# A fourth k chunk with seven products in eight late pairs, and an added transfer for two weight halves of each

## The chip, the cores and the metric

The kernel runs on one core of one Trainium2 chip. The metric is the device time in microseconds of one execution. The kernel before took 1013.76, 1014.27 and 1014.4 us in three runs, median 1014.27 us.

## The reference

The program is one layer of a bidirectional encoder on `x` of 256 x 2048 float32 (batch 1). The normalised input is multiplied with one wide weight `w_in`, whose columns are cut into the parts of two branches and two gates; each branch is projected by a 2048 x 2048 weight, the two are merged by the gates, and an output projection and a last RMSNorm follow:

```python
h = _rms_norm(x, norm_g)
proj = jnp.einsum('bsd,dn->bsn', h, w_in.astype(h.dtype))
...
q_p, k_p, v_p, o_p, za_p, gif_p, xb_p, zb_p, ga_p, gb_p = jnp.split(proj, cuts, axis=-1)
ya = _mlstm_branch(q_p, k_p, v_p, o_p, za_p, gif_p, b_if, head_g)
yb = _rglru_branch(xb_p, zb_p, conv_w, conv_b, w_rg, b_rg, lam)
ya = jnp.einsum('bsw,wd->bsd', ya, w_branch_a.astype(ya.dtype))
yb = jnp.einsum('bsw,wd->bsd', yb, w_branch_b.astype(yb.dtype))
merged = (jax.nn.sigmoid(ga_p.astype(jnp.float32)) * ya.astype(jnp.float32)
          + jax.nn.sigmoid(gb_p.astype(jnp.float32)) * yb.astype(jnp.float32)).astype(x.dtype)
return x + jnp.einsum('bsd,de->bse', merged, w_out.astype(x.dtype))
```

What concerns the change are five products of a 256 x 2048 activation with 2048 x 2048 weights late in the program: `yb @ w_branch_b`, the gates `gb` and `ga` (columns of `w_in`), `ya @ w_branch_a`, and then `merged @ w_out`.

## The kernel before, in words

**Products in two parts.** A float32 operand is kept as two tiles of the type that TensorE multiplies here: `hi` (the rounded value) and `lo` (the value less `hi`). A product is three matmuls, a·hi, a·lo and b·hi, where a and b are the activation's two parts. Each is 128 x 128 by 128 x 512.

**A plain chunk.** A weight block has 512 columns and eight k chunks of 256 rows (`KC` = 2 tiles of 128). `load_chunk` (L125) brings one chunk of a block, 128 x 1024 or 512 KB, on SyncE's queue (L134) to a `raw` tile of six, ScalarE casts it to `whi` (L140), and VectorE subtracts to `wlo` (L141). Each has four buffers. A plain chunk of one block is 12 matmuls, two k tiles by two row blocks by three; one of both blocks is 24.

**A pair.** `pair` (L163) computes two blocks at once. Its eight matmul groups end in two accumulators of two PSUM banks each (`acc`). At some k chunks, the "product" chunks, `products` (L184) forms quarter sums of the four 256 x 256 sub-blocks by VectorE (L199, L200, L203, L204) and does seven products in place of eight, 21 matmuls in place of 24. Three products go straight to the accumulators and four to extra banks, `aux` p1, p5, p7 and p6, which hold sums over all product chunks of the pair. The transfers of such a chunk are L190 and L191, its casts L180, its low halves L181. Beside the weights it needs "forms", the same quarter sums of the activation, made ahead by `make_form` (L271 to L285) into slots of SBUF. Which chunks are products and at which of the eight places they are worked is given by the tables `S_..` and `L_..`.

**The end of a pair.** When the last product chunk is done, the aux banks are combined in the result tile: ScalarE copies p1 (L252), then VectorE adds p6 (L253), p7 (L254) and p5 twice (L255, L256). L253 needs both p6 and the copy of p1. The plain chunks left over follow, first all of the first half, then of the second. After each half VectorE adds its accumulator (L262), and what the pair is for follows (for a gate a sigmoid on ScalarE, then a multiply at L957; for the last pairs L988 and L989). [...]

**The eight late pairs.** They are, in order: `wb` twice (WB0, WB1 here), gate b twice (GB0, GB1), gate a twice (GA0, GA1) and `wa` twice (WA0, WA1). Each has three product chunks, kq 0, 2 and 4 at places 0, 2 and 4 (in WA1 at 1, 3 and 5), so 3 x 21 + 5 x 24 = 183 matmuls. After the last product chunk three plain chunks of each half are left over (two in WA1). Then comes `block_nat` (L145) for `wo[2]`, a block alone, whose chunks are preceded by transposes of the merged result (L981) with their low half by VectorE (L336), then a pair for `wo[0]` and `wo[1]` with four product chunks, and `wo[3]`.

**What sets the order.** The instructions of one engine run in the order in which the tile scheduler put them, each after the semaphores of what it reads and of the buffer that it overwrites. `with urgent()` gives the loads, casts and evictions a higher priority. A row that waits on its engine holds up all rows behind it.

## Time and profile before

| | |
|---|---|
| times | 1013.76, 1014.27, 1014.4 us, median 1014.27 us |
| profiled execution | span 1012.2 us from the first to the last instruction, 2.1 us less than the median |
| TensorE busy | 1003.0 us, 99% |
| VectorE busy | 875.8 us, 87% |
| ScalarE busy | 628.6 us, 62% |
| GpSimd busy | 18.6 us, 2% |
| 16 DMA engines of q1, where the weights come in | 58.9% |
| mean granted TensorE clock | 0.998 |
| start of L253, the first add of the aux banks, in WB0, WB1, GB0, GB1, GA0, GA1, WA0, WA1 | 607.9, 649.9, 691.3, 732.9, 774.3, 815.3, 856.8, 905.2 us |
| start of L253 in the pair of `wo` | 978.3 us |

Busy shares are of the whole span. In the names of a row, what is written stands left of the arrow and what is read right of it, each a tile's name; the shapes are partitions x elements. A slot's tile is named for the slot (sE, sD), an accumulator acc, an extra bank aux. Consecutive rows of one engine overlap a little: an instruction's duration is longer than the distance to the next one's start.

### The profile page before, as it was taken

Reading aid. Unit: us, or ns where it says so; the run is one execution under the profiler, and the core shown is the slowest. Engines: PE = TensorE matmul, PEld = TensorE weight load, DVE = VectorE, ACT = ScalarE, POOL = GpSimd, SP = SyncE. Lnnn points to the kernel's source line nnn. Section 1 sums busy time; section 2 is a strip of 40 time slices with the busy share of each in tenths; the row PEclk is TensorE's granted clock in tenths of the full one; section 3 lists DMA queues with packets and bytes.
Section 4 is the critical chain, followed back from the end, with each engine's and each line's share of the span. In section 5 each row is a group of like instructions: output and inputs, shape, how many; then the busy total and the mean of one; then the engine's idle time right before and its main releaser. Section 6 shows DMA issues by size and latency. Waiting matters only on the chain.

```text
span 1012.2 us, 13718 instructions
## 1 busy us (share of the span) xinstructions
PE 1003.0 (99%) x5045; PEld 853.2 (84%) x5045; DVE 875.8 (87%) x1167; ACT 628.6 (62%) x825; POOL 18.6 (2%) x37
## 2 busy tenths in 40 slices
PE   9999999999999999999999999999999999999997
...
DVE  6687898889769888997697888998898988999996
...
GB/s 349 263 208 157 160 153 198 173 213 197 167 190 167 177 197 184 210 167 227 146 199 208 155 208 188 212 212 201 187 216 200 219 177 212 184 217 336 161 200 83
DMA packets 56387, 199.32 MB, mean 197 GB/s; under 512 B 6400, under 2 KB 7424, under 8 KB 55936
## 3 DMA queue, kind: packets, MB, share of 16 engines
q1 hardware_dynamic: 55456, 197.13, 58.9%
...
## 4 chain that ended last, share of the span: by engine, by line
PE 97%; DVE 1%; DMA 1%; ACT 0%; issue 0%; ACTq 0%; SPq 0%; DVEq 0%
PE acc L176 17%; PE acc L177 17%; PE acc L174 17%; PE acc L315 16%; PE acc L318 8%; PE aux L176 3%; PE aux L174 3%; PE aux L177 3%; PE aux L855 1%; PE aux L721 1%; PE aux L720 1%; PE aux L719 1%; PE aux L1053 1%; PE aux L1052 1%; PE aux L1051 1%; PE acc L156 1%
## 5 line engine op out<-in xcount | busy, mean ns | idle before, releaser
L140 ACT CAST whi<-raw 128x1024 fp32r<-128x1024 f32 (+1 forms) x284 | 294.8, 1046 | 196.0 <-PE acc L177 99.7
L141 DVE TENSOR_TENSOR wlo<-raw,whi 128x1024 fp32r<-128x1024 f32 (+1 forms) x284 | 341.5, 1213 | 76.2 <-ACT whi L140 74.4
L176 PE MATMUL acc<-wlo,sHL 128*128 128x512 f32 x554 | 215.9, 390 | 0.0
L177 PE MATMUL acc<-whi,sHL 128*128 128x512 f32 x554 | 215.8, 390 | 0.0
L174 PE MATMUL acc<-whi,sHL 128*128 128x512 f32 x554 | 213.3, 390 | 0.0
L315 PE MATMUL acc<-sHL,whi 128*128 128x512 f32 x704 | 175.9, 393 | 0.0
L315 PEld LDWEIGHTS acc<-sHL,whi 128*128 128x128 f32 x704 | 127.4, 189 | 23.5
L174 PEld LDWEIGHTS acc<-whi,sHL 128*128 128x128 f32 x554 | 104.0, 188 | 21.2
L176 PEld LDWEIGHTS acc<-wlo,sHL 128*128 128x128 f32 x554 | 104.1, 188 | 21.0
L177 PEld LDWEIGHTS acc<-whi,sHL 128*128 128x128 f32 x554 | 104.0, 188 | 20.9
L318 PEld LDWEIGHTS acc<-sHL,wlo 128*128 128x128 f32 x704 | 95.3, 190 | 6.0
L180 ACT CAST whi<-t 128x1024 fp32r<-128x1024 f32 x70 | 73.5, 1051 | 42.9 <-PE acc L177 13.9
L318 PE MATMUL acc<-sHL,wlo 128*128 128x256 f32 x704 | 99.0, 283 | 0.0
L181 DVE TENSOR_TENSOR wlo<-t,whi 128x1024 fp32r<-128x1024 f32 x70 | 85.5, 1222 | 9.0 <-ACT whi L180 8.5
L180 ACT CAST whi<-raw 128x1024 fp32r<-128x1024 f32 x37 | 39.0, 1053 | 27.6 <-PE acc L177 16.9
L181 DVE TENSOR_TENSOR wlo<-raw,whi 128x1024 fp32r<-128x1024 f32 x37 | 45.2, 1222 | 8.7 <-ACT whi L180 8.7
L180 ACT CAST b<-raw 128x512 fp32r<-128x512 f32 x28 | 17.4, 621 | 39.2 <-DMA raw<-wi 16.5
L176 PE MATMUL acc<-wlo,sC 128*128 128x512 f32 x92 | 35.9, 390 | 0.4 <-DVE wlo L141 0.4
L176 PE MATMUL acc<-wlo,sA 128*128 128x512 f32 x92 | 36.0, 392 | 0.0
L177 PE MATMUL acc<-whi,sD 128*128 128x512 f32 x92 | 35.8, 389 | 0.0
L177 PE MATMUL acc<-whi,sB 128*128 128x512 f32 x92 | 35.8, 389 | 0.0
L174 PE MATMUL acc<-whi,sC 128*128 128x512 f32 x92 | 35.3, 389 | 0.0
...
## 6 DMA issues: line engine op xcount, KB each, us to landing
raw<-wi SPq DMA_DIRECT2D x254, 512.0 KB, 4.2
raw<-wb SPq DMA_DIRECT2D x32, 512.0 KB, 4.1
raw<-wa SPq DMA_DIRECT2D x32, 512.0 KB, 4.0
raw<-wo SPq DMA_DIRECT2D x32, 512.0 KB, 4.8
raw<-wr SPq DMA_DIRECT2D x8, 512.0 KB, 4.0
sB<-x SPq DMA_DIRECT2D x4, 512.0 KB, 7.7
sA<-x SPq DMA_DIRECT2D x1, 2048.0 KB, 7.9
...
```

The source lines that it names most:

```text
L140: last_copy[0] = act.copy(hi[:, r], raw[:, r]).ins
L141: last_sub[0] = dve.tensor_sub(lo[:, r], raw[:, r], f(hi[:, r])).ins
L156: pe.matmul(ps[tb], a, wl, start=False, stop=False)
L174: pe.matmul(ps, a, wh, start=id(ps) not in began, stop=False)
L176: pe.matmul(ps, a, wl, start=False, stop=False)
L177: pe.matmul(ps, b, wh, start=False, stop=stop)
L180: act.copy(hi, v)
L181: dve.tensor_sub(lo, v, f(hi))
L315: pe.matmul(ps[m], hi[:, o:o + P], hl_t[:, 2 * k * S:2 * (k + 1) * S], start=(k == 0), stop=(turn and k == KT - 1), skip_group_check=True)
L318: pe.matmul(ps[m][:, :S], lo[:, o:o + P], hhi(k * S, (k + 1) * S), start=False, stop=(not turn and k == KT - 1), skip_group_check=True)
L719: pe.matmul(dst, whi[:, o:o + P], xh[:, r], start=True, stop=False)
L720: pe.matmul(dst, whi[:, o:o + P], xl[:, r], start=False, stop=False)
```

## The change

All eight late pairs have four product chunks, kq 0, 2, 4 and 6 at these places, so one plain chunk (kq 7) of each half is left over behind the last of them. A new function `load_added` takes the second block's chunk at kq 3 and at kq 7 of each pair: the raw chunk is brought and cast as before (`ahi`), ScalarE writes the negated high half to `alo`, and a transfer on GpSimd's queue reads the same chunk from HBM and adds it onto `alo`, which then holds the low half. VectorE has no part in these 16 chunks. The loads of kq 3 are issued ahead of place 0, those of kq 7 ahead of place 4. `ahi` takes the buffer "zz", which was one of two for the high and low half of b11 (the first of the quarter blocks); b11 keeps the one buffer "to". Forms for kq 6 are added, forms are made at other places, and eight small tiles move to slot E.

```diff
@@ -24,12 +24,13 @@
 EPS = 1e-6
 NEG = -1e30
 
-S_WB, S_GB, S_GA, S_WA = [((0, 2, 4), (0, 2, 4))] * 4
+S_WB, S_GB, S_GA, S_WA = [((0, 2, 4, 6), (0, 2, 4, 6))] * 4
 S_OZ = (((4, 0), (2, 4)), ((4,), (1,)), ((4, 0), (2, 5)), ((4, 0), (0, 2)))
 S_V = (((4,), (4,)), ((4,), (4,)))
 S_WO = (0, 1, 2, 4)
-L_WB, L_GB, L_GA, L_WA = ((0, 2, 4), (0, 2, 4)), ((0, 2, 4), (0, 2, 4)), ((0, 2, 4), (0, 2, 4)), ((0, 2, 4), (1, 3, 5))
+L_WB, L_GB, L_GA, L_WA = [((0, 2, 4, 6), (0, 2, 4, 6))] * 4
 L_WO = (0, 2, 4, 6)
+ADDED = ((0, 3), (4, 7))
 H_FORMS = (4, 0)
 PLAN = (dict(Y=('c0', '', '', 'c1',),
              V=('', '', 'c2 c3', 'g0', '', '', 'g1', '', '', '', 'g2 g3',),
@@ -141,6 +142,17 @@
                 last_sub[0] = dve.tensor_sub(lo[:, r], raw[:, r], f(hi[:, r])).ins
         return hi, lo
 
+    def load_added(src):
+        with urgent():
+            raw = wp.tile([P, KC * NB], F32, tag="raw", name=name("raw"), bufs=6)
+            hi = hp.tile([P, KC * NB], F32R, tag="zz", name=name("ahi"))
+            lo = hp.tile([P, KC * NB], F32R, tag="alo", name=name("alo"))
+            sp.dma_start(raw, src)
+            act.copy(hi, raw)
+            act.mul(lo, f(hi), -1.0)
+            pool.dma_start(lo, src, accum_op=ALU.add)
+        return hi, lo
+
     def block_nat(src, xhi, xlo):
         ps, _ = acc_pair()
         for kq in range(KT // KC):
@@ -160,7 +172,7 @@
     def four(v):
         return v.rearrange("p (a b) -> p a b", b=S)
 
-    def pair(src, xhi, xlo, forms, kqs, dst, b11, epilogue, sums=None, places=None, calm=False):
+    def pair(src, xhi, xlo, forms, kqs, dst, b11, epilogue, sums=None, places=None, calm=False, added=()):
         aps = []
         accs = [acc_pair()[1] for _ in range(2)]
         banks = [[v[:, :NB], v[:, NB:]] for v in accs]
@@ -227,7 +239,7 @@
             mm(banks[1][0], *sf(3), h3[:, lf], l3[:, lf], False)
 
         def plain(kq, jj):
-            hi, lo = load_chunk(src[jj][kq])
+            hi, lo = ready.pop((kq, jj)) if (kq, jj) in ready else load_chunk(src[jj][kq])
             for kk in range(KC):
                 o = (kq * KC + kk) * S
                 c = slice(kk * NB, (kk + 1) * NB)
@@ -236,7 +248,15 @@
                        hi[:, c], lo[:, c], kq == kl and kk == KC - 1)
 
         last = max(places)
+        ready = {}
+
+        def ahead(i):
+            for a, b in added:
+                if a == i:
+                    ready[seq[b], 1] = load_added(src[1][seq[b]])
+
         for i, kq in enumerate(seq[:last + 1]):
+            ahead(i)
             if kq in kqs:
                 products(kq, i == last)
             else:
@@ -447,7 +467,7 @@
         pool.memset(t, 0.0)
     gn = ct([P, 2, 16], "gn")
     NS = 48
-    cat, ab, ey, sv, qv, pv, ng, spl = (ct([P, NS], n) for n in ("cat", "ab", "ey", "sv", "qv", "pv", "ng", "spl"))
+    cat, ab, ey, sv, qv, pv, ng, spl = (et([P, NS]) for _ in range(8))
     c8, c4 = ct([P, 32], "c8"), ct([P, 32], "c4")
     an = et([P, 2, P])
     negM, em = ct([P, 2, 8], "negM"), ct([P, 2, 8], "em")
@@ -910,9 +930,6 @@
 
     k_yb, k_h, k_ya = (sorted(set(sum(v, ()))) for v in (S_WB, S_GB + S_GA, S_WA))
     k_h = [kq for kq in k_h if kq not in hf]
-    early = [lambda kq=kq, i=i: h_form(kq, i) for kq, i in zip(k_h, (3, 0, 1))]
-    early += [lambda kq=kq, i=i: ya_form(kq, i) for kq, i in zip(k_ya[:1], (3, 0, 1)[len(early):])]
-
     for j in range(4):
         for i in range(2):
             both = half_tr(wi[BLK_ZB + j], i)
@@ -933,22 +950,20 @@
         for kq in (2 * j, 2 * j + 1):
             if kq in k_yb:
                 form("b", kq, k_yb.index(kq), full=sg[:, (kq % 2) * NB:(kq % 2 + 1) * NB])
-        if j == 1:
-            early[0]()
     ybh, ybl = Cols(ybh, 1024), Cols(ybl, 1024)
     nb11 = [0]
 
     def b11():
         nb11[0] += 1
-        v = hp.tile([P, 2 * NB], F32R, tag=("to", "zz")[nb11[0] % 2], name=name("b11"))
+        v = hp.tile([P, 2 * NB], F32R, tag="to", name=name("b11"))
         return v[:, :NB], v[:, NB:]
 
     sgb = sl("E")
     sgv = [sgb[:, j * 1024:(j + 1) * 1024] for j in range(4)]
     for p in range(2):
-        pair((wb[2 * p], wb[2 * p + 1]), ybh, ybl, forms("b"), S_WB[p], sgv[2 * p:2 * p + 2], b11, lambda jj: None, None, L_WB[p])
-    for fn in early[1:]:
-        fn()
+        pair((wb[2 * p], wb[2 * p + 1]), ybh, ybl, forms("b"), S_WB[p], sgv[2 * p:2 * p + 2], b11, lambda jj: None, None, L_WB[p], added=ADDED)
+    for i, kq in enumerate(k_h):
+        h_form(kq, i)
     for p in range(2):
         gb = [sl(f"D{2 * p + i}", F32, 1024) for i in range(2)]
 
@@ -956,7 +971,8 @@
             act.activation(gb[jj], gb[jj], AF.Sigmoid)
             dve.tensor_mul(sgv[2 * p + jj], sgv[2 * p + jj], gb[jj])
 
-        pair((wi[BLK_GB + 2 * p], wi[BLK_GB + 2 * p + 1]), hhi, hlo, forms("h"), S_GB[p], gb, b11, epi_gb, None, L_GB[p])
+        pair((wi[BLK_GB + 2 * p], wi[BLK_GB + 2 * p + 1]), hhi, hlo, forms("h"), S_GB[p], gb, b11, epi_gb, None, L_GB[p], added=ADDED)
+        ya_form(k_ya[p], 2 + p)
     ga = []
     for p in range(2):
         ga += [sl(f"C{2 * p + i}", F32, 1024) for i in range(2)]
@@ -964,9 +980,10 @@
         def epi_ga(jj, p=p):
             act.activation(ga[2 * p + jj], ga[2 * p + jj], AF.Sigmoid)
 
-        pair((wi[BLK_GA + 2 * p], wi[BLK_GA + 2 * p + 1]), hhi, hlo, forms("h"), S_GA[p], ga[2 * p:], b11, epi_ga, None, L_GA[p])
-    for i, kq in enumerate(k_ya[1:]):
-        ya_form(kq, 1 + i)
+        pair((wi[BLK_GA + 2 * p], wi[BLK_GA + 2 * p + 1]), hhi, hlo, forms("h"), S_GA[p], ga[2 * p:], b11, epi_ga, None, L_GA[p], added=ADDED)
+    for kq, slot_ in zip(k_ya[2:], H_FORMS[::-1]):
+        fslot["a", kq] = halves(sl(f"F{slot_}", F32R, 1024), 0)
+        make_form(fslot["a", kq], parts=[t(kq * NB, (kq + 1) * NB) for t in (yah, yal)])
 
     m_t = sl("HL", F32R, 8192)
     mh, ml = Cols([m_t[:, :4096]], 4096), Cols([m_t[:, 4096:]], 4096)
@@ -991,7 +1008,7 @@
                 queue.extend([None] * (1 - p))
                 queue.extend([lambda i=i, h=h: fin_m(i, h) for i in (2 * p, 2 * p + 1) for h in range(2)])
 
-        pair((wa[2 * p], wa[2 * p + 1]), yah, yal, forms("a"), S_WA[p], wd, b11, epi_wa, None, L_WA[p], calm=True)
+        pair((wa[2 * p], wa[2 * p + 1]), yah, yal, forms("a"), S_WA[p], wd, b11, epi_wa, None, L_WA[p], calm=True, added=ADDED)
 
     y = sl("A")
     fgt = sl("PT")
```

In the new file L253 to L256 are L273 to L276, L252 is L272, L262 is L282, L141 is L142, L181 is L193, L190 and L191 are L202 and L203, L199, L200, L203 and L204 are L211, L212, L215 and L216, L336 is L356, L988 and L989 are L1005 and L1006, and L981 is L998. `load_added` casts at L151, negates at L152 and adds at L153.

VectorE's order where WB0 ends and WB1 begins, before (aux_1184 to aux_1187 and acc_1170 are WB0's; tiles from raw_1258 on belong to WB1):

```order
L253 TENSOR_TENSOR sE_1169_5557<-aux_1187_5588,sE_1169_5557 128x512
L141 TENSOR_TENSOR wlo_1236_5799<-raw_1234_5797,whi_1235_5798 128x1024
L254 TENSOR_TENSOR sE_1169_5557<-aux_1186_5587,sE_1169_5557 128x512
L141 TENSOR_TENSOR wlo_1240_5817<-raw_1238_5815,whi_1239_5816 128x1024
L255 TENSOR_TENSOR sE_1169_5557<-aux_1185_5586,sE_1169_5557 128x512
L256 TENSOR_TENSOR sE_1169_5557<-aux_1185_5586,sE_1169_5557 128x512
L141 TENSOR_TENSOR wlo_1245_5836<-raw_1243_5834,whi_1244_5835 128x1024
L199 TENSOR_TENSOR t_1261_5898<-raw_1258_5891 128x512
L181 TENSOR_TENSOR b11_1260_5895<-raw_1258_5891,b11_1260_5895 128x512
L200 TENSOR_TENSOR t_1261_5898<-raw_1259_5892,raw_1258_5891 128x512
L141 TENSOR_TENSOR wlo_1249_5854<-raw_1247_5852,whi_1248_5853 128x1024
L203 TENSOR_TENSOR t_1262_5899<-t_1261_5898,raw_1258_5891 128x512
```

and after the change (aux_1188 to aux_1191, acc_1170 and acc_1171 are WB0's; raw_1266 and raw_1267 are WB1's first product chunk, raw_1290 and raw_1291 its second):

```order
L273 TENSOR_TENSOR sE_1169_5548<-aux_1191_5586,sE_1169_5548 128x512
L193 TENSOR_TENSOR b11_1268_5905<-raw_1266_5901,b11_1268_5905 128x512
L274 TENSOR_TENSOR sE_1169_5548<-aux_1190_5585,sE_1169_5548 128x512
L212 TENSOR_TENSOR t_1293_5994<-raw_1291_5988,raw_1290_5987 128x512
L142 TENSOR_TENSOR wlo_1284_5953<-raw_1282_5951,whi_1283_5952 128x1024
L275 TENSOR_TENSOR sE_1169_5548<-aux_1189_5584,sE_1169_5548 128x512
L276 TENSOR_TENSOR sE_1169_5548<-aux_1189_5584,sE_1169_5548 128x512
L215 TENSOR_TENSOR t_1294_5995<-t_1293_5994,raw_1290_5987 128x512
L193 TENSOR_TENSOR b11_1292_5991<-raw_1290_5987,b11_1292_5991 128x512
L282 TENSOR_TENSOR sE_1169_5548<-sE_1169_5548,acc_1170_5549 128x1024
L282 TENSOR_TENSOR sE_1169_5548<-sE_1169_5548,acc_1171_5550 128x1024
```

Between the first and the last aux row three subtractions of plain chunks stood; a b11 and a plain chunk's subtraction stand there now, and an L212 that reads the second raw tile of WB1's second product chunk. The accumulators follow directly on the four aux rows.

ScalarE's order at the same place, before:

```order
L180 CAST b11_1219_5732<-raw_1217_5728 128x512
L180 CAST whi_1222_5739<-t_1220_5735 128x1024
L180 CAST whi_1224_5745<-t_1221_5736 128x1024
L180 CAST whi_1226_5749<-raw_1218_5729 128x1024
L140 CAST whi_1231_5780<-raw_1230_5779 128x1024
L252 COPY sE_1169_5557<-aux_1184_5585 128x512
L140 CAST whi_1235_5798<-raw_1234_5797 128x1024
L140 CAST whi_1239_5816<-raw_1238_5815 128x1024
L140 CAST whi_1244_5835<-raw_1243_5834 128x1024
L180 CAST b11_1260_5895<-raw_1258_5891 128x512
```

and after:

```order
L192 CAST b11_1243_5813<-raw_1241_5809 128x512
L192 CAST whi_1271_5912<-t_1269_5908 128x1024
L192 CAST whi_1273_5918<-t_1270_5909 128x1024
L192 CAST whi_1275_5922<-raw_1267_5902 128x1024
L151 CAST ahi_1263_5895<-raw_1262_5894 128x1024
L272 COPY sE_1169_5548<-aux_1188_5583 128x512
L192 CAST b11_1268_5905<-raw_1266_5901 128x512
L152 ACTIVATE alo_1264_5896<-ahi_1263_5895 128x1024
L141 CAST whi_1283_5952<-raw_1282_5951 128x1024
L192 CAST b11_1292_5991<-raw_1290_5987 128x512
```

The copy of p1 (aux_1184 before, aux_1188 after) now stands behind the three casts of WB1's first product chunk and behind ahi_1263, the cast of WB1's added chunk for kq 3, which overwrites the buffer of WB0's added chunk for kq 7 (ahi_1218). SyncE's transfer to raw_1291 waits on ScalarE: it overwrites the tile that ahi_1263 is cast from.

VectorE's order where WA1 has ended and `block_nat` runs on `wo[2]`, before (sHL holds the merged result's two halves, xp a form's sums; the third row is the add of WA1's second accumulator, acc_1779):

```order
L336 TENSOR_TENSOR sHL_1688_7585<-aux_1853_8214,sHL_1688_7585 128x512
L989 TENSOR_TENSOR sC2_1601_7236<-sC2_1601_7236,sE_1169_5557 128x1024
L262 TENSOR_TENSOR sD3_1777_7924<-sD3_1777_7924,acc_1779_7926 128x1024
L141 TENSOR_TENSOR wlo_1897_8381<-raw_1895_8379,whi_1896_8380 128x1024
L988 TENSOR_TENSOR sC3_1602_7237<-sC3_1602_7237,sD3_1777_7924 128x1024
L141 TENSOR_TENSOR wlo_1901_8399<-raw_1899_8397,whi_1900_8398 128x1024
L989 TENSOR_TENSOR sC3_1602_7237<-sC3_1602_7237,sE_1169_5557 128x1024
L141 TENSOR_TENSOR wlo_1905_8417<-raw_1903_8415,whi_1904_8416 128x1024
L336 TENSOR_TENSOR sHL_1688_7585<-aux_1874_8297,sHL_1688_7585 128x512
L336 TENSOR_TENSOR sHL_1688_7585<-aux_1880_8322,sHL_1688_7585 128x512
L285 TENSOR_TENSOR sE_1914_8475<-xp_1236,sE_1914_8475 128x512
L199 TENSOR_TENSOR t_1923_8515<-raw_1920_8508 128x512
```

and after, the rows that end with the low half of the fifth of eight transposed pieces (aux_1920):

```order
L212 TENSOR_TENSOR t_1957_8625<-raw_1955_8619,raw_1954_8618 128x512
L300 TENSOR_TENSOR xp_1228<-xp_1228 128x128
L302 TENSOR_TENSOR xp_1228<-xp_1228 128x128
L142 TENSOR_TENSOR wlo_1931_8495<-raw_1929_8493,whi_1930_8494 128x1024
L215 TENSOR_TENSOR t_1958_8626<-t_1957_8625,raw_1954_8618 128x512
L301 TENSOR_TENSOR xp_1228<-xp_1228 128x128
L142 TENSOR_TENSOR wlo_1937_8520<-raw_1935_8518,whi_1936_8519 128x1024
L216 TENSOR_TENSOR t_1958_8626<-raw_1955_8619,t_1958_8626 128x512
L303 TENSOR_TENSOR xp_1228<-xp_1228 128x128
L142 TENSOR_TENSOR wlo_1943_8545<-raw_1941_8543,whi_1942_8544 128x1024
L297 TENSOR_TENSOR xp_1228<-sHL_1714_7671 128x512
L356 TENSOR_TENSOR sHL_1714_7671<-aux_1920_8461,sHL_1714_7671 128x512
```

Before, the low half of the fifth piece (aux_1874) stood six rows behind the add of WA1's second accumulator, with no form and no quarter sum between. After the change it stands 23 rows behind it (aux_1920), and ten of the rows between are of forms (L297 to L303) and quarter sums (L211 to L216).

## The prediction

> **What bounds the kernel now.** I read the page's busy rows first, then the chain that ended last, then what TensorE waited for over the whole run, then windows of the eight pairs.
>
> ```profile
> PE 1003.0 (99%) x5045; PEld 853.2 (84%) x5045; DVE 875.8 (87%) x1167; ACT 628.6 (62%) x825; POOL 18.6 (2%) x37
> ...
> DVE  6687898889769888997697888998898988999996
> ...
> PE 97%; DVE 1%; DMA 1%; ACT 0%; issue 0%; ACTq 0%; SPq 0%; DVEq 0%
> ```
>
> TensorE (PE) is busy in 99% of the span of 1012.2 us and makes 97% of the chain. VectorE (DVE) is no spectator: in the last third of the slices it is busy to 80% and more.
>
> ```profile
> PE aux L345 <- DVE wu L377: 1.1, 1, 1.1
> PE acc L303 <- DVE wlo L141: 0.8, 2, 0.6
> PE acc L176 <- DVE wlo L141: 0.4, 1, 0.4
> ```
>
> Those are all the waits of TensorE (total us, times, longest), 2.3 us, and just 0.4 of it in the line of the late pairs. So today TensorE sets the end alone, and whatever keeps it from issuing is new.
>
> ```profile
> 733.00:774.00 41.00, 41.00 (x183) 33.95 (x182) 37.57 (x42) 23.29 (x25) 0.00 (x0) 1.00 0.63 205
> ...
> 857.00:905.00 48.00, 48.00 (x218) 39.69 (x217) 45.30 (x54) 24.83 (x27) 0.00 (x0) 1.00 0.58 194
> 905.00:977.00 72.00, 72.00 (x334) 59.85 (x333) 69.05 (x90) 41.63 (x52) 0.00 (x0) 1.00 0.66 237
> ```
>
> Columns: length, then busy us of PE, PEld, DVE, ACT and POOL, TensorE's granted clock (1.00), the share of the DMA engines, GB/s. In a pair (first row) DVE is at 92%, in the last two at 94 and 96%, with PE at 100%. ScalarE (ACT) has 40% free.
>
> **The gain.** Each pair has one plain chunk less and one product chunk more: 24 matmuls become 21.
>
> ```profile
> 699.78 0.39 PE L174 MATMUL acc<-whi,sHL 128*128 128x512 f32 x1
> ...
> 701.14 0.39 PE L176 MATMUL acc<-wlo,sHL 128*128 128x512 f32 x1
> ```
>
> The second row is six matmuls behind the first: 1.36 / 6 = 0.227 us each. Eight pairs save 8 x 3 x 0.2267 = **5.4 us**, if TensorE never waits.
>
> **What it costs VectorE.** Its rows where WB0 ends:
>
> ```profile
> 607.90 0.69 DVE L253 TENSOR_TENSOR sE<-aux,sE 128x512 f32<-128x512 f32 x1 [0.56 <-PE acc L177]
> 608.51 1.22 DVE L141 TENSOR_TENSOR wlo<-raw,whi 128x1024 fp32r<-128x1024 f32 x1
> 609.64 0.68 DVE L254 TENSOR_TENSOR sE<-aux,sE 128x512 f32<-128x512 f32 x1
> ...
> 611.97 0.68 DVE L256 TENSOR_TENSOR sE<-aux,sE 128x512 f32<-128x512 f32 x1
> ...
> 618.98 1.22 DVE L262 TENSOR_TENSOR sE<-sE,acc 128x1024 f32<-128x1024 f32 x1
> ```
>
> From start to start a 512 row takes 0.60 us (607.90 to 608.51) and a 1024 row 1.13 us (608.51 to 609.64). A product chunk has five of the first kind and three of the second, 6.42 us; the plain chunk that goes took 2.27, and the two added chunks take 2.27 off. VectorE gets 6.42 - 2.27 - 2.27 = 1.9 us more in every pair, and TensorE 0.7 us less. On 37.6 of 41 us that is 39.5 of 40.3: 98%. The added transfers pay for a good half of the fourth product chunk, not for all of it.
>
> **The tail.** Here I choose where the money is. Before, L262 came 11 us after L253 (618.98 against 607.90), because three plain chunks of the first half lie between. During these, TensorE needs no bank of the next pair, and DVE empties the four aux banks at ease. After the change one plain chunk of each half is left, 24 matmuls of 0.227 = 5.4 us, and the next pair asks for the same banks at once. I count from T, the start of the last matmul that writes p6's bank. In TensorE's new order at WB0 | WB1 the next pair's first matmul into p5's bank is 45 rows behind T (10.2 us), its first into an accumulator 50 rows behind (11.3 us).
>
> Against that stand the orders of DVE and ACT shown above. p1's last matmul is 29 rows behind T and ends at T + 6.8, later than p6's. Its copy on ACT (L272) ends 0.6 later, and L273 needs that copy: it starts at about T + 7.5. The rows up to the end of L276 are b11, L274, L212, L142, L275, L276, 5 x 0.60 + 1.13 = 4.1 us, and L273 itself 0.6: p5 is free at T + 12.2 if nothing else waits. But L212 reads raw_1291. That transfer waits for the cast of ahi_1263, and this cast for the buffer that WB0's added chunk is read from, to the 21st row behind T, T + 5.0. With a cast of 1.05 us it is issued at T + 6.4. What such a transfer takes stands in the rows
>
> ```profile
> raw<-wi SPq DMA_DIRECT2D x254, 512.0 KB, 4.2
> raw<-wb SPq DMA_DIRECT2D x32, 512.0 KB, 4.1
> ...
> sA<-x SPq DMA_DIRECT2D x1, 2048.0 KB, 7.9
> ...
> sPT<-fg SPq DMA_DIRECT2D x1, 1024.0 KB, 7.6
> ```
>
> (issues of transfers: KB each, median us to landing) and of ACT at the same place
>
> ```profile
> 605.98 0.58 ACT L252 COPY sE<-aux 128x512 f32<-128x512 f32 x1
> 606.46 1.05 ACT L140 CAST whi<-raw 128x1024 fp32r<-128x1024 f32 x1
> ```
>
> At 4.1 us it lands at T + 10.5. Then L212, L142, L275 and L276 follow, 3 x 0.60 + 1.13 = 2.9 us, and with the semaphores p5 is free at T + 13.7: 3.5 us late. L215, b11 and L282 come next, 0.60 + 0.60 + 1.13 = 2.3, so the accumulator is free at T + 16.0, 4.7 us after it was asked for. Bounds: 3 us, if the transfer is early and the L273 chain alone decides (12.2 + 2.3 = 14.5 against 11.3), and 6 us if it takes 1.3 us longer. I take **4.7 us** for WB0 | WB1.
>
> At the other six boundaries of pairs p1 is done 7.3 to 8.6 us before T, so L273 starts with T; I let it end at T + 1.2. The same count of DVE rows against PE rows gives for the first accumulator, free against asked for: WB1 | GB0 11.4 and 10.7 us, GB0 | GB1 9.4 and 10.7, GB1 | GA0 11.1 and 10.7, GA0 | GA1 11.1 and 10.9, GA1 | WA0 and WA0 | WA1 9.4 and 11.1. That is 0.7 + 0.4 + 0.2 = 1.3, with 0.3 for low halves of weights that come a tenth late: **1.6 us**. Bounds 0 and 2.8. In the trace L253 ended 1.5 us behind the start of its bank's last matmul (608.59 less 607.05, the row below), but was put down to a later one:
>
> ```profile
> 607.05 0.39 PE L177 MATMUL aux<-whi,sPT 128*128 128x512 f32 x1
> ```
>
> 0.3 more at each of these four terms makes 2.8. Nothing is left if the four come 0.3 to 0.7 sooner than counted.
>
> **WA1 and the lone block behind it.** The fifth transposed piece is DVE row 31 counted from L273. Ahead of it, with L273, lie 12 rows of 1024, 15 of 512 and 4 small ones.
>
> ```profile
> 930.81 0.28 DVE L280 TENSOR_TENSOR xp<-xp 128x128 f32<-128x128 f32 x1
> 931.01 0.29 DVE L282 TENSOR_TENSOR xp<-xp 128x128 f32<-128x128 f32 x1
> ...
> 912.03 0.60 PE L981 MATMUL aux<-ident,sC 128*128 128x128 f32 x4
> 912.38 0.48 PE L176 MATMUL acc<-wlo,sA 128*128 128x512 f32 x1
> ```
>
> They take 13.6 + 9.0 + 0.8 = 23.4 us, and the piece 0.7: it is there at T + 24.6. TensorE reaches the matmul that reads it after 82 matmuls and seven groups of transposes (0.4 each, the last two rows), T + 21.4. Rows from WA1's accumulators to `wo`'s evictions add up to 68.3 us on DVE against 66.1 on PE, so 2.2 is lost there anyhow. I take **3.0 us**, bounds 2.2 and 4.
>
> **The added transfers.** The trace holds no accumulating transfer. It reads 512 KB and what lies in SBUF, and writes: three times the traffic at most, so 4.1 us from below, 3 x 4.2 = 12.6 from above. I take 7.9, which the rows of 1 and 2 MB gave. Between PE's release of the buffers and its first read of `alo` lie 15.2 to 18.8 us in the new order, of which ACT's cast and negation (two of 1.05 us and their queue) take 2.5 to 3.6: 11.7 us are left in the tightest place but the first (8.4 us). It costs nothing at 7.9; POOL has no other row then. On ACT a pair gets two negations and 1.7 us of casts more, 3.8 us on 23.3 of 41. Transfers go from 32 to 34 a pair, the share from 0.63 to about 0.67.
>
> [...]
>
> **Sum.** -5.4 + 4.7 + 1.6 + 3.0 = +3.9 us. On the profiled span of 1012.2 that is 1016.1; the median lies 2.1 above that execution, so **1018.2 us**.
>
> **Rivals.** *The stalls are covered (faster).* The place is WB0 | WB1: if raw_1291's slot is free before the cast of ahi_1263, L212 does not wait and 3 us are lost there; and a pause of TensorE lets DVE run ahead, so that the small terms and WA1's vanish. -5.4 + 3.0 = -2.4: 1011.9. It decides when all waits together stay below 3.4 us. For it speaks that DVE at 96% (905 to 977) left PE without a wait; against it, that both large terms are counted from T in rows that cannot start before T. Chance 0.17.
>
> *Only one of the two binds (no change).* WB0 | WB1 at 4.7 and WA1 hidden, or 3.0 and 2.2 with nothing between: -0.7 to -0.2, 1013.6 to 1014.1. Chance 0.25.
>
> *The added transfer lands late (slower).* If it takes over 12 us, each of 15 waits for `alo` costs the excess: 14 us give 2 x 15 = 30 on top, 1048. The row for 512 KB speaks against it by a factor of three. [...] Chance 0.08.
>
> *Every boundary costs some 3 us (slower).* DVE at 98% has no slack to make good a late transfer; seven boundaries x 3 with 3.0 in WA1 gives -5.4 + 24 = +19, 1033. The longest list of ACT's waits for a transfer between 600 and 980 us speaks for it,
>
> ```profile
> ACT b L180 <- DMA raw<-wi: 16.5, 11, 2.7
> ```
>
> the PE waits so far against: eleven such waits reached TensorE nowhere. Chance 0.1.
>
> *My case:* 0.4, own range 1016.3 to 1023.
>
> **Range and chances.** About 0.2% (2.0 us) is what a measurement can tell from no change: faster is below 1012.2, slower above 1016.3. Faster 0.18, from the first rival; same 0.26, from the second; slower 0.56, mine less a little and the last two. The range runs from 1011 (first rival with another 0.9 saved) to 1028 (half of the boundary rival).
>
> **What would show it.** Right: TensorE waits of about 9 us in all, against 2.3; at WB0 | WB1 one on DVE's L276 or L282 and DVE's L212 waiting for raw from `wb`; at `wo[2]` one on L356; `alo` landing 5 to 9 us after its issue. Wrong: no such waits (first rival), waits on L153 all along (third), or waits of 2 to 4 us at each boundary (fourth). A span 5 us shorter would say that the count of rows from T is worth nothing.

## The result, and the profile after

The changed kernel takes 1055.42 us (median of 3 runs, 1055.2 to 1056.75) against 1014.27: ratio 1.0415, 95% interval 1.0399 to 1.0432. It is slower by 41 us, where 4 were forecast. The profiled execution has a span of 1053.7 us, 41.5 more than before, and is the one that the rows below come from. One of the four executions of e8 below took 2038.57 us at full granted clock; why is not known, and it is left out of that run's numbers.

The page of the changed kernel: busy rows, TensorE's granted clock in 40 slices, and the chain that ended last by engine.

```profile
PE 1018.3 (97%) x5021; PEld 856.6 (81%) x5021; DVE 897.1 (85%) x1216; ACT 653.7 (62%) x860; POOL 32.6 (3%) x53
...
PEclk9999999999999999999999999899989999999999
...
PE 19%; DVE 10%; DMA 8%; issue 2%; ACT 1%; DVEq 0%; ACTq 0%
```

TensorE has the 24 matmuls less that the change promised (5045 to 5021), and is still busy for 15 us longer: its matmuls have become slower. The chain can be followed back only to 626 us, 40% of the span; in these 40%, DVE and DMA have 10 and 8, where they had 1% each of the whole span before.

What TensorE waited for (total us, times, longest us), the seven longest of 16 rows that sum to 28.2 us, against 2.3 before:

```profile
PE aux L186 <- ACT b L192: 5.5, 3, 4.1
PE acc L186 <- DVE sD L282: 4.0, 3, 1.9
PE acc L169 <- DVE sHL L356: 3.6, 1, 3.6
PE acc L186 <- DVE sE L282: 2.6, 2, 2.1
PE acc L188 <- DVE wlo L193: 2.5, 1, 2.5
PE aux L186 <- DVE sD L276: 2.1, 1, 2.1
PE acc L186 <- DVE sC L282: 1.9, 1, 1.9
```

L276 and L282 are the emptying of the aux banks and of the accumulators: in these rows the next pair's matmuls into them waited for VectorE's reads, up to 2.1 us at a time. The first row is for the cast of the next b11 (`b`) on ScalarE. The longest wait of that row, 4.1 us until 917.15, is for a cast that itself stood 7.2 us for a load from `wa`; between 600 and 960 us ScalarE waits 56.1 us for loads of raw tiles, against 35.8 before. The waits are spread over the ends of all the pairs. What follows one of them stands in TensorE's timeline where WB1 ends:

```profile
679.93 0.79 PE L186 MATMUL acc<-whi,sHL 128*128 128x512 f32 x1 [2.13 <-DVE sE L282]
680.53 0.63 PE L188 MATMUL acc<-wlo,sHL 128*128 128x512 f32 x1
680.95 0.63 PE L189 MATMUL acc<-whi,sHL 128*128 128x512 f32 x1
...
684.37 0.63 PE L186 MATMUL acc<-whi,sHL 128*128 128x512 f32 x1
684.79 1.06 PE L186 MATMUL aux<-whi,sPT 128*128 128x512 f32 x2
685.65 0.55 PE L188 MATMUL acc<-wlo,sHL 128*128 128x512 f32 x1
```

After a pause of 2.13 us the matmuls start every 0.43 us in place of 0.227, for nearly 6 us, before they go at full pace again. The windows show it as granted clock (columns as in the prediction; the clock is 0.85 in the first and 1.00 in the second):

```profile
680.00:700.00 20.00, 20.00 (x76) 16.21 (x77) 16.39 (x22) 8.90 (x10) 0.00 (x0) 0.85 0.63 200
...
700.00:720.00 20.00, 20.00 (x89) 16.50 (x88) 17.76 (x22) 13.02 (x16) 0.87 (x1) 1.00 0.77 237
```

TensorE is "busy" for all of the first 20 us and does 76 matmuls, where the next 20 us hold 89.

The drops of the granted clock stand on a grid of 3.41 us in the trace: from 560 us on they begin at 627.94, 679.14, 771.30, 819.09, 918.08 and 959.03 us, whole multiples of 3.413 us apart. Stretches of that grid around the pause above, and one around a pause of 2.51 us at 896.00 (length, busy us of PE and its matmuls, granted clock, DMA share, GB/s):

```profile
672.31:675.72 3.41, 3.00 (x14) 1.00 0.14 58
675.73:679.14 3.41, 1.30 (x5) 1.00 0.46 154
679.14:682.55 3.41, 2.62 (x6) 0.50 0.88 198
682.55:685.96 3.41, 3.41 (x9) 0.50 1.00 285
685.97:689.38 3.41, 3.41 (x16) 1.00 0.71 282
...
894.18:897.59 3.41, 1.59 (x7) 1.00 0.19 60
```

In these six places (without the end of the program) the clock stands at 0.50 for 27.3 us in all. Ahead of each of them TensorE had paused for 2.0 to 2.9 us within one stretch of the grid; 1.8 us, as in the last row, was not enough here. So a pause that the grid cuts in two can pass (here 2.51 us, of which 1.82 lie in one stretch), and two shorter ones in one stretch can do it (0.77 and 1.33 us from 675.73 on).

**Where the 41.5 us are.** I went through all starts of TensorE from 560 us on and added up what each was later than 0.227 us (less for smaller forms). The sum is 46.6 us in the changed kernel and 1.0 before. Of the 46.6, 26.8 are pauses, 17.4 are 92 starts that were late by half a matmul (0.11 us) or more beyond the pause ahead of them, if any, and 2.4 is the rest. Of the 92, some 60 lie where the granted clock is 0.50 and are worth 13 us; the others stand at full clock, most of them right behind a pause, and are 0.1 to 0.2 us late each. 46.6 less 1.0 less the 5.4 saved is 40.2, of 41.5 measured. By place, pauses and late starts together:

| place | us | forecast |
|---|---|---|
| WB0, WB1 | 6.1 | 4.7 |
| WB1, GB0 | 6.9 | 0.7 |
| GB0, GB1, and within GB1 | 2.6 | 0 |
| GB1, GA0 | 7.3 | 0.4 |
| GA0, GA1 | 4.3 | 0.2 |
| last chunks of WA0 | 2.8 | 0.3, with all low halves |
| WA0, WA1 and WA1's first chunk | 8.7 | 0 |
| WA1, `wo[2]` | 6.1 | 3.0 |

### The profile page after: what moved, and what is told of

Same layout as the page of the kernel before. It is cut to its first block, busy times and chain, and to the rows that moved or that the text cites. A ratio compares the mean times of both kernels' runs of the same rounds, so it can differ in the third digit from the quotient of the medians.

```text
span 1053.7 us, 13816 instructions
## 1 busy us (share of the span) xinstructions
PE 1018.3 (97%) x5021; PEld 856.6 (81%) x5021; DVE 897.1 (85%) x1216; ACT 653.7 (62%) x860; POOL 32.6 (3%) x53
## 5 line engine op out<-in xcount | busy, mean ns | idle before, releaser
L141 ACT CAST whi<-raw 128x1024 fp32r<-128x1024 f32 (+1 forms) x252 | 260.9, 1043 | 174.7 <-PE acc L189 75.8
L142 DVE TENSOR_TENSOR wlo<-raw,whi 128x1024 fp32r<-128x1024 f32 (+1 forms) x252 | 303.5, 1212 | 71.6 <-ACT whi L141 70.0
L186 PE MATMUL acc<-whi,sHL 128*128 128x512 f32 x498 | 196.0, 397 | 6.3 <-DVE sD L282 2.3
L188 PE MATMUL acc<-wlo,sHL 128*128 128x512 f32 x498 | 197.1, 396 | 0.1
L189 PE MATMUL acc<-whi,sHL 128*128 128x512 f32 x498 | 196.7, 395 | 0.0
L193 DVE TENSOR_TENSOR wlo<-t,whi 128x1024 fp32r<-128x1024 f32 x86 | 104.3, 1220 | 11.0 <-ACT whi L192 10.4
L188 PEld LDWEIGHTS acc<-wlo,sHL 128*128 128x128 f32 x498 | 95.1, 191 | 20.1 <-DVE wlo L142 0.5
L193 DVE TENSOR_TENSOR wlo<-raw,whi 128x1024 fp32r<-128x1024 f32 x45 | 54.9, 1220 | 1.9 <-ACT whi L192 1.9
L211 DVE TENSOR_TENSOR t<-raw 128x512 f32<-128x512 f32 x41 | 28.3, 689 | 22.4 <-DMA raw<-wi 13.9
L212 DVE TENSOR_TENSOR t<-raw,raw 128x512 f32<-128x512 f32 x41 | 28.1, 687 | 7.8 <-DMA raw<-wa 5.1
L216 DVE TENSOR_TENSOR t<-raw,t 128x512 f32<-128x512 f32 x45 | 30.9, 687 | 0.3
L193 DVE TENSOR_TENSOR b<-raw,b 128x512 fp32r<-128x512 f32 x36 | 24.7, 687 | 4.8 <-ACT b L192 4.8
L215 DVE TENSOR_TENSOR t<-t,raw 128x512 f32<-128x512 f32 x41 | 28.1, 686 | 0.1
```

What stands on the lines that cost most here:

```text
L141: last_copy[0] = act.copy(hi[:, r], raw[:, r]).ins
L142: last_sub[0] = dve.tensor_sub(lo[:, r], raw[:, r], f(hi[:, r])).ins
L186: pe.matmul(ps, a, wh, start=id(ps) not in began, stop=False)
L188: pe.matmul(ps, a, wl, start=False, stop=False)
L189: pe.matmul(ps, b, wh, start=False, stop=stop)
L193: dve.tensor_sub(lo, v, f(hi))
```

## The experiments

Two theories at first. **A**: VectorE has no slack left and the tail behind the last product chunk is too short to empty the four aux banks and both accumulators. **B**: the added chunks' single buffers hold SyncE's queue. The changed kernel's list of waits of SyncE's queue has such a row, beside the usual ones for a free raw tile:

```profile
SPq L134 <- DVE wlo L142: 351.5, 158, 9.9
...
SPq L134 <- ACT ahi L151: 47.4, 10, 7.0
```

All kernels were timed beside the kernel before on the same chip (1013.4 to 1014.6 us); the differences in the table further down are to that. The altered kernels spread more than that one, by up to 8 us in four executions (e3, e5, e13).

### e1_three_added

```diff
-S_WB, S_GB, S_GA, S_WA = [((0, 2, 4, 6), (0, 2, 4, 6))] * 4
-L_WB, L_GB, L_GA, L_WA = [((0, 2, 4, 6), (0, 2, 4, 6))] * 4
+S_WB, S_GB, S_GA, S_WA = [((0, 2, 4), (0, 2, 4))] * 4
+L_WB, L_GB, L_GA, L_WA = ((0, 2, 4), (0, 2, 4)), ((0, 2, 4), (0, 2, 4)), ((0, 2, 4), (0, 2, 4)), ((0, 2, 4), (1, 3, 5))
```

> The changed kernel with three product chunks in each pair as before (places 0, 2, 4; WA1 1, 3, 5); the added transfers, the one buffer for b11 and the placing of forms stay. Theory A (the tail is too short: with one plain chunk of each half behind the last product chunk VectorE cannot empty the banks in time, and late transfers only follow from that): the 72 matmuls of the tail are back, VectorE has 2.3 us a pair less than before, TensorE waits less than 4 us in all, 1011 to 1017 us. Theory B (the queue is blocked: the raw tile of an added chunk is free only after its cast, the cast waits for the one high-half buffer, and SyncE's queue stands for it, 47.4 us in ten waits in the changed kernel): the same ten or so waits of SyncE on line 151's cast, transfers late, TensorE waits 10 us or more, 1025 us or more.

1020.86 us, ratio 1.0077 (1.0059 to 1.0094). TensorE waits 4.5 us, most of it at WB0 | WB1. Neither number is quite hit. The added transfers, with the one b11 buffer and the new places of the forms, are a loss even where VectorE has 2.3 us a pair less to do than before the change, though a small one. The new places alone were not tried; this run bounds what they can cost with three product chunks at some 7 us. SyncE's queue stood 38 us for line 151 here too, with hardly a wait of TensorE. That speaks against B as the main cost.

### e2_four_plain

```diff
-ADDED = ((0, 3), (4, 7))
+ADDED = ()
```

> The changed kernel with four product chunks and no added transfers: the 16 chunks are loaded and subtracted like all others. VectorE then has 4.15 us a pair more than before, 41.7 us against 40.8 us of matmuls. Theory A: the boundaries wait as in the changed kernel or longer, and VectorE is over by 1 us a pair on top: 1055 to 1075 us. Theory B: nothing stands in SyncE's queue, so only VectorE's excess of some 8 to 11 us is left against the 5.4 us saved: 1015 to 1030 us.

1046.02 us, ratio 1.0322 (1.0305 to 1.034): between the two. VectorE has 1.1 us more for each of 16 chunks, and yet the kernel is 9 us faster than the changed one. Its waits are behind lines 282 and 276 as well. So the fourth product chunk costs some 30 us without any added transfer (e8 below has it with two b11 buffers), and the transfers cost more than the 18 us of VectorE's time that they save are worth.

### e3_own_raw and e7_raw_on_pool

```diff
-            raw = wp.tile([P, KC * NB], F32, tag="raw", name=name("raw"), bufs=6)
+            raw = wp.tile([P, KC * NB], F32, tag="rawx", name=name("raw"), bufs=1)
...
-            sp.dma_start(raw, src)
+            pool.dma_start(raw, src)
```

The first hunk, with five raw tiles for all other loads, is e3; both are e7.

> The changed kernel, but the raw tile of an added chunk is a buffer of its own and the other transfers share five in place of six: a cast that waits for the high-half buffer no longer holds a tile that SyncE's next transfers want. Theory A: the waits of TensorE stay at 20 us and more, 1045 to 1060 us. Theory B: SyncE's waits on line 151's cast go from 47 us to below 10, TensorE waits less than 12 us, 1015 to 1030 us. If five tiles are too few, transfers come later everywhere and the run says nothing for B.

> The changed kernel, but the raw tile of an added chunk is a buffer of its own (five are left for the others) and its transfer is issued by GpSimd, so nothing of the added chunks stands in SyncE's queue; e3_own_raw only moved that wait to line 150. Theory A: TensorE waits 20 us and more, 1040 to 1060 us. Theory B: waits of SyncE on line 151's cast are gone, TensorE waits below 12 us, 1015 to 1030 us.

e3 takes 1059.65 us (1.0453, 1.0421 to 1.0484). It tells nothing of B, since the wait only moved to the added load itself (46.5 us of waits at line 150). In e7 no row of SyncE waits for line 151, and it takes 1060.6 us (1.0458, 1.044 to 1.0475), TensorE waiting over 30 us. Both times are at the upper end of theory A's answers or just above. One tile less may cost something in both, but with the block gone nothing was won.

### e4_long_tail

```diff
-L_WB, L_GB, L_GA, L_WA = [((0, 2, 4, 6), (0, 2, 4, 6))] * 4
+L_WB, L_GB, L_GA, L_WA = [((0, 1, 2, 4), (0, 1, 2, 4))] * 4
```

> The changed kernel with its four product chunks at places 0, 1, 2 and 4, so three plain chunks of each half (72 matmuls) follow the last of them, as before the change; the added transfers stay (places 3 and 7). Theory A: the waits at the ends of pairs vanish; three product chunks on end may cost some waits for low halves at the start of a pair (6.4 us of VectorE against 4.8 us of matmuls for each): 1008 to 1025 us. Theory B: SyncE's queue is blocked as it was: 1040 us or more.

1040.56 us, ratio 1.0265 (1.025 to 1.0281). TensorE's waits in this kernel:

```profile
PE aux L186 <- ACT whi L192: 5.4, 9, 0.9
PE aux L188 <- DVE wlo L193: 3.7, 7, 1.5
...
PE acc L186 <- DVE sE L282: 0.3, 1, 0.3
```

With 72 matmuls behind the last product chunk, the waits for lines 276 and 282 fall from 11.7 to 0.3 us: the short tail is why TensorE waits at the ends of the pairs. But the same lack then shows at the next place, where three product chunks on end want their low halves. The sum of pauses falls only from 26.8 to 14.4 us. The late starts stay at 15.4 us, but most of them are now short delays behind many short pauses: the clock is at 0.50 for 10.2 us in place of 27.3, which is worth 5 of the 15.4. At 1040.56 us the run is above theory A's 1025, so the tail is not all of it.

### e5_free_low and e6_no_plain_low

```diff
-                last_sub[0] = dve.tensor_sub(lo[:, r], raw[:, r], f(hi[:, r])).ins
+                if not nolo:
+                    last_sub[0] = dve.tensor_sub(lo[:, r], raw[:, r], f(hi[:, r])).ins
...
-            hi, lo = ready.pop((kq, jj)) if (kq, jj) in ready else load_chunk(src[jj][kq])
+            hi, lo = load_chunk(src[jj][kq], nolo=jj == 1 and kq in [seq[b] for _, b in added])
```

This is e5, without the loads ahead; with `nolo`, `lo` is the tile of `hi`. In e6 `nolo` holds for every plain chunk of the late pairs.

> The changed kernel, but the low halves of the 16 added chunks are left out: these chunks are loaded and cast like all others and the matmuls read the high half in the low half's place, so no negation, no added transfer and no single buffer for them; that part of the sum is left out of the result. VectorE's work is that of the changed kernel (39.5 us a pair by the prediction's count). Theory A (VectorE at 98% and a tail of 24 matmuls): the waits behind lines 276 and 282 stay, 1030 to 1050 us. Theory B (the added chunks' single buffers block SyncE's queue): none is left, 1010 to 1020 us.

> As the run before, but the low halves of all eight plain chunks of each late pair are left out, so VectorE has 6.8 us a pair less still: about 33 of 40.8 us. The short tail stays. If the shortness of the tail is the cost by itself, waits behind lines 276 and 282 stay and the time is above 1020 us. If it is VectorE's lack of slack, the waits are gone and the 5.4 us saved shows: 1007 to 1012 us.

e5: 1034.06 us, ratio 1.0197 (1.0168 to 1.0225), as theory A has it. e6: 1023.06 us, 1.009 (1.0067 to 1.0112): neither of the two answers, since the time is above 1020 us but most of the waits are gone. With 6.8 us a pair less on VectorE, the waits behind lines 276 and 282 are nearly all at WB0 | WB1 (4.8 us there with the late starts), and what else is left are waits of about 1.1 us for a product chunk's low half in three pairs. VectorE's work is worth 11 us between these two runs. That the rest of the fourth chunk's cost lies in how late its loads come is a guess.

### e8_plain_two_b11

```diff
-        v = hp.tile([P, 2 * NB], F32R, tag="to", name=name("b11"))
+        v = hp.tile([P, 2 * NB], F32R, tag=("to", "zz")[nb11[0] % 2], name=name("b11"))
```

on top of e2's edit.

> As e2_four_plain (no added transfers, 1046 us), with b11 alternating between two buffers as before the change. If the one b11 buffer matters, the waits for b (4.4 us of TensorE's waits there) go and the time falls by 5 to 10 us with the clock's share; if VectorE alone sets it, 1042 to 1048 us.

1043.07 us, ratio 1.03 (1.0283 to 1.0317), against e2's 1.0305 to 1.034. The time is in the range given for VectorE alone. The one b11 buffer is worth some 2 to 3 us here at most, as the two intervals overlap.

### e9_no_transfer, e10_one_high_buffer and e11_high_own_raw

Between e5 and the changed kernel lie 21 us: all that the added chunks bring beside the relief of VectorE. Two theories were left for them: **C**, the transfers themselves, and **D**, the tiles held for the one high-half buffer.

```diff
             sp.dma_start(raw, src)
             act.copy(hi, raw)
             act.mul(lo, f(hi), -1.0)
-            pool.dma_start(lo, src, accum_op=ALU.add)
```

This is e9. e10 drops the negation too and sets `lo = hi`; e11 is e10 with e7's two edits, but with six raw tiles for the rest.

> The changed kernel without the 16 added transfers alone: the raw load, the cast to the one high-half buffer and the negation stay, and the matmuls read the negated high half as low half, so the source is not added and the result lacks that. Between e5_free_low (1034 us, no single buffers and no transfers) and the changed kernel (1055 us) lie 21 us. Theory C (traffic and latency of the added transfers make the other transfers late): 1032 to 1038 us. Theory D (a raw tile that is held until the one high-half buffer is free delays the transfers that want it): 1048 to 1056 us.

> As e9_no_transfer, and without the negation: the matmuls read the high half in the low half's place. What is left of the added chunks is the load ahead of its use, the raw tile of the six and the one high-half buffer. Theory D: 1045 to 1056 us, VectorE waits over 20 us for raw as in the changed kernel (27.4 us there, 9.0 in e5_free_low). If ScalarE's 16 negations are what costs, 1032 to 1040 us while e9_no_transfer is at 1048 or more.

> As e10_one_high_buffer, but the raw tile of an added chunk is a buffer beside the six, and GpSimd issues its load: neither a tile of the six nor SyncE's queue waits for the high-half buffer. (e7_raw_on_pool had only five tiles for the rest.) Theory D: the waits for raw go back to some 9 us and the time to that of e5_free_low, 1028 to 1038 us. If it stays with e10_one_high_buffer within 4 us, neither the tile nor the queue is the cause; then ScalarE, which stands still in the cast of the high half until TensorE has read the one before, is what is left.

1032.56 us (1.0186, 1.0166 to 1.0206), 1034.92 us (1.0208, 1.0192 to 1.0223) and 1027.78 us (1.0139, 1.0104 to 1.0174). In e9 and e10 the times are those of e5: a load ahead, one high-half buffer and the negations cost nothing that can be seen, and theory C holds: the transfers alone are worth 22 us (41.2 against 19.2). Theory D falls as the cause of these 22 us, but it is not nothing: e11 is 7 us below e10, clear of both intervals, and VectorE's waits for raw between 600 and 960 us fall from 13.3 to 4.4 us. So a seventh raw tile, loaded by GpSimd, helps where there are no added transfers; which of the two edits does it was not tried. Some rows stand in another order in e9 than in the changed kernel (77 of 1216 on VectorE), which e13 does not share.

### e13_transfer_no_add and e14_eight_added

```diff
-            pool.dma_start(lo, src, accum_op=ALU.add)
+            pool.dma_start(lo, src)
```

This is e13, in which every engine has the changed kernel's order; the transfer overwrites the low half, so the matmuls read the whole source there. In e14 only the pair (0, 3) of `ADDED` is loaded by `load_added`, and kq 7's second chunk is loaded without a low half.

> The changed kernel with every instruction in the same order; only the 16 transfers to the low half overwrite it in place of adding, so the matmuls read the whole source there. If adding is what costs (the added transfers took 8.6 us from issue to landing where plain ones took 4.2): transfers land after 4 to 5 us, the time is between e9_no_transfer and the changed kernel and nearer the former, 1033 to 1042 us. If 512 KB more in each of 16 places is enough: 1047 to 1056 us.

> The changed kernel with the added transfer for the chunk of kq 3 of each pair alone; the second half's chunk of kq 7 is loaded and cast as all others are, its low half is left out (the matmuls read the high half), so VectorE's work stays that of the changed kernel and eight transfers are left. If the cost goes by the number of transfers, half of the 21 to 23 us between e5_free_low or e9_no_transfer and the changed kernel: 1042 to 1046 us. If the transfer for kq 7, which runs while the next pair's loads begin, is the one that hurts: 1034 to 1039 us.

e13: 1036.18 us, ratio 1.0205 (1.018 to 1.0231), so +21.6: the same bytes brought by the same instructions cost 2 us more than none (e9; the intervals overlap), and that they are added costs the other 20. The transfers landed after 6.0 us (median of 16), not after 4 to 5 as expected. e14: 1041.68 us, 1.0267 (1.0249 to 1.0285), +27.1: about a third of the way from e9 or e5 to the changed kernel, just below what was expected if it went by number, and above the answer for kq 7 alone. The second eight transfers cost about twice what the first did.

What adding does to the queues stands in the DMA view from 600 to 950 us (packets, MB, share of the 16 engines' time; then KB each and median us to landing). The changed kernel:

```profile
q1 hardware_dynamic: 17954, 65.92, 55.4%
q0 software_dynamic: 2160, 7.87, 12.2%
...
raw<-wi SPq DMA_DIRECT2D x64, 512.0 KB, 4.6
raw<-wa SPq DMA_DIRECT2D x32, 512.0 KB, 5.4
raw<-wb SPq DMA_DIRECT2D x19, 512.0 KB, 4.7
alo<-wi POOLq DMA_DIRECT2D x8, 512.0 KB, 8.6
```

and e13:

```profile
q0 software_dynamic: 2160, 7.87, 7.3%
...
alo<-wi POOLq DMA_DIRECT2D x8, 512.0 KB, 6.7
```

q1 moves 1 MB in 0.84% of the engines' time, q0 takes 1.55% when it adds and 0.93% when it doesn't. For 512 KB (0.524 MB) in these 350 us that is 1.5, 2.8 and 1.7 us of all 16 engines. The raw loads of the pairs landed after 4.2 to 4.4 us in e9 (medians by weight), 4.5 to 4.6 in e13 and 4.6 to 5.4 in the changed kernel, and VectorE, whose rows stand in a fixed order, waits for them. Its longest waits for raw tiles between 600 and 960 us in the changed kernel:

```profile
DVE t L211 <- DMA raw<-wi: 13.3, 7, 3.2
...
DVE t L212 <- DMA raw<-wa: 5.1, 4, 2.3
```

and before the change:

```profile
DVE t L199 <- DMA raw<-wa: 1.1, 1, 1.1
```

In all it waits 27.4 us for raw tiles in the changed kernel, 19.5 in e13, 16.5 in e9, 9.4 in e5 and 2.8 before the change. That the longer packets of q0 (0.32 us each in the changed kernel, 0.19 in e13, from the shares and counts above) are what makes the other loads late is read from these views together and was not tried by itself; that adding costs the 20 us is what e13 shows.

### e12_two_pairs

On the kernel before:

```diff
-S_WB, S_GB, S_GA, S_WA = [((0, 2, 4), (0, 2, 4))] * 4
+S_WB, S_GB, S_GA, S_WA = ((0, 2, 4), (0, 2, 4)), ((0, 2, 4), (0, 2, 4)), ((0, 2, 4, 6), (0, 2, 4, 6)), ((0, 2, 4), (0, 2, 4))
```

with the same in `L_GA`, and one form in another slot.

> The kernel before with a fourth product chunk (kq 6 at place 6) in the two pairs of gate a alone, loaded and subtracted as all chunks are, b11 in two buffers, one more form of gate chunks. TensorE saves 1.4 us, VectorE gets 4.15 us more in each of two pairs that had 36 to 38 of 41 us. If the cost is that VectorE's backlog grows from pair to pair, two pairs between pairs with slack cost little: 1012 to 1017 us. If each short tail costs by itself as in e2_four_plain (32 us over eight pairs, 4 us a pair): 1019 to 1023 us.

1013.42 us, ratio 1.0 (0.999 to 1.001). Two short tails between pairs with slack cost nothing: TensorE waits 0.4 us in all the late pairs. Its profiled span is 1011.3 us, 0.9 below that of before, of 1.4 saved; in the times nothing can be told. So in this place a short tail costs nothing where VectorE comes to it without work left over, with slack on both sides of the two pairs; the other six pairs were not tried alone. No run was faster than the kernel before by what can be measured.

### All runs together

Change in us to the kernel before; then, from 560 us on in the profiled execution, pauses of TensorE, number of late starts as defined above, what these cost, and how long the granted clock stood at 0.50 (without the end of the program). The profiled execution was 4.8 us below the median in e5, and above it by 4.6 in e13, 4.4 in e7 and 2.9 in e11.

| run | change | pauses | late starts | cost of these | clock at 0.50 |
|---|---|---|---|---|---|
| changed kernel | +41.2 | 26.8 | 92 | 17.4 | 27.3 |
| e1 three products, added | +7.3 | 3.1 | 7 | 1.0 | 0 |
| e2 four, no added | +32.5 | 21.6 | 77 | 14.0 | 20.5 |
| e3 own raw | +46.1 | 28.9 | 96 | 18.5 | 30.7 |
| e4 long tail | +27.0 | 14.4 | 91 | 15.4 | 10.2 |
| e5 16 low halves free | +20.5 | 14.3 | 37 | 5.9 | 3.4 |
| e6 all plain low halves free | +9.5 | 8.2 | 34 | 5.7 | 3.4 |
| e7 raw by GpSimd | +47.0 | 31.9 | 115 | 20.1 | 23.9 |
| e8 four, no added, two b11 | +29.5 | 22.8 | 59 | 10.5 | 17.1 |
| e9 added without transfer | +19.2 | 13.7 | 45 | 8.7 | 13.7 |
| e10 one high buffer | +21.5 | 15.1 | 53 | 9.6 | 13.7 |
| e11 with own raw | +14.4 | 10.1 | 55 | 10.3 | 17.1 |
| e12 two pairs | 0.0 | 0.4 | 3 | 0.4 | 0 |
| e13 transfer without adding | +21.6 | 19.2 | 62 | 11.0 | 13.7 |
| e14 eight added | +27.1 | 19.5 | 61 | 11.8 | 17.1 |

## Why the prediction was wrong

The direction was right; the size was a tenth. The two large terms came out near in size, but not by the waits that the prediction had put there. The time lies outside the range, above both slower rivals (1033 and 1048).

**The gain**: 24 matmuls less, as counted. In e12, where nothing else is in the way, the profiled span is 0.9 us shorter of 1.4, which is inside the spread of the times, so the gain itself was not measured.

**WB0 | WB1**: 4.7 forecast, 6.1 measured, and the nearness is luck. Rows of VectorE there:

```profile
625.72 0.69 DVE L211 TENSOR_TENSOR t<-raw 128x512 f32<-128x512 f32 x1 [1.01 <-DMA raw<-wb]
626.33 1.22 DVE L193 TENSOR_TENSOR wlo<-raw,whi 128x1024 fp32r<-128x1024 f32 x1
627.46 0.69 DVE L273 TENSOR_TENSOR sE<-aux,sE 128x512 f32<-128x512 f32 x1
...
629.26 0.68 DVE L212 TENSOR_TENSOR t<-raw,raw 128x512 f32<-128x512 f32 x1
...
631.60 0.68 DVE L276 TENSOR_TENSOR sE<-aux,sE 128x512 f32<-128x512 f32 x1
```

L212 did not wait for raw_1291. The copy of p1, which was to hold L273 back, had ended at 625.82, 1.6 us before L273 began; VectorE was late, with L211 waiting for a transfer ahead of the whole eviction. Of the 6.1 us the waits that the term priced, for L276 and then for L282, are 0.8 us (0.35 and 0.49). The rest are pauses of 1.31 us for L273 and 0.93 us for a cast on ScalarE, a short one for the low half of that cast, and 2.8 us of late starts.

**The step that failed first: "L273 starts with T".** The six other boundaries were counted as if VectorE had nothing left over when the last aux matmul comes. Here is the end of WB1 before the change, its last matmul into p6's bank and the first add:

```profile
649.01 0.39 PE L177 MATMUL aux<-whi,sPT 128*128 128x512 f32 x1
...
649.92 0.68 DVE L253 TENSOR_TENSOR sE<-aux,sE 128x512 f32<-128x512 f32 x1
```

and after it, the same matmul on TensorE, and VectorE's rows up to the first add:

```profile
665.10 0.39 PE L189 MATMUL aux<-whi,sPT 128*128 128x512 f32 x1
```

```profile
662.92 0.69 DVE L211 TENSOR_TENSOR t<-raw 128x512 f32<-128x512 f32 x1 [1.55 <-DMA raw<-wi]
...
668.81 0.69 DVE L273 TENSOR_TENSOR sE<-aux,sE 128x512 f32<-128x512 f32 x1
```

668.81 less 665.10 is 3.7 us. At the seven ends from WB1 to WA1 the distance is 3.7, 2.9, 4.7, 3.0, 1.6, 7.1 and 1.5 us; before the change it was 0.6 to 1.1 at the same places, in e12 0.7 to 1.1, and in e9, without the transfers, 0.6 to 2.7. The count behind L273 held: from L273's start to the end of the first L282 the six boundaries take 11.0, 8.7, 10.5, 10.5, 8.7 and 8.7 us, against 10.9, 8.9, 10.6, 10.6, 8.9 and 8.9 by the prediction's figures, and VectorE waits for nothing in between. So the start failed and not the rows behind it. In e2 it is the other way round: L273 starts 0.6 to 2.1 us behind the same matmul, but up to 13.0 us of rows, with the subtractions that the transfers would have taken over, lie between it and the end of L282. The sum of VectorE's rows gave 39.5 of 40.3 us; as an average that leaves 0.8 us a pair for every wait of VectorE. One late load of 1.55 us uses that up. The rival of a wait at every boundary had this mechanism; its 3 us a place were close to the pauses (26.8 over the eight places of the table), and 0.1 was too low a chance for it.

**The step that failed second: "It costs nothing at 7.9".** Landing after 7.9 us was a good guess (8.6, from 6.3 to 10.4) and TensorE never waited for `alo` in the changed kernel. What the text priced was the transfer's own lateness. Its cost lies elsewhere, as far as the views show in what it does to the others: 2.8 us of all 16 engines where a plain load takes 1.5, while the loads of product chunks are due. By e9 and e13 that is 20 to 22 of the 41 us, and more than the relief of VectorE is worth (12 to 13 us, e2 against e5 and e9). The rival of late added transfers missed it as well, since it let only TensorE wait.

That GpSimd issues these transfers is the smaller part of it. In e13 GpSimd issues the same 16 without adding: they landed after 6.0 us (median) against 8.6, took 1.7 us of all 16 engines against 2.8, and the run costs 2 us more than e9, with intervals that overlap. Adding decided here.

**The term that was missing: the clock.** The sum counted a pause as its length. In the trace pauses of 26.8 us brought 17.4 us of late starts, 13 of them at half clock. Not each pause does: behind 2.13 us at 679.93 it was 13 matmuls at 0.43 us, behind 2.51 at 896.00 and 1.75 at 907.21 none.

In the stretch of the grid from 675.73 on, pauses of 2.1 of 3.41 us were enough: half pace (0.43 against 0.227 us a matmul) followed. I had read that the clock stood at 1.00 in the windows before the change, and did not ask what it would do once there were pauses.

**WA1 and `wo[2]`**: 3.0 us forecast within 2.2 to 4; the wait for L356 was 3.6 and one for L355 0.3, and late starts behind them made it 6.1. The sign was right, the place was not. The forecast's wait was for the fifth transposed piece. The trace's wait ends at 958.26 with the second, whose L356 starts at 957.52 behind both adds of WA1's accumulators, a subtraction, L1005 and L211; the fifth piece's L356 starts at 970.76, and TensorE does not wait for it. That the size fits is luck.

**WB0 | WB1 in the runs**: it costs 4.0 to 9.1 us in each of e2, e5, e6, e8, e9, e10 and e11, pauses and late starts together, so this boundary is a real term. The late p1 is not shown as its cause: L273 waited for the copy only in e2 and e11, for 0.3 and 0.4 us; in the others the copy had ended 2.5 us or more before L273 began, and VectorE was at rows ahead of it. (The text on the orders counts three subtractions between the first and the last aux row before the change; the rows show two there.)

What stays open is how the 19 us of a fourth chunk without added transfers (e9) divide between VectorE's lack of slack and late loads, since the loads in turn wait for raw tiles that VectorE frees (the first SPq row above): e6 takes VectorE's load away and keeps 9.5 us, of which 4.8 are WB0 | WB1. It also stays open why one seventh raw tile is worth 7 us in e11. And it was not tried whether an added transfer that is issued when no product chunk's loads are due would cost less.
